# Seven-product couples first, plain couples last, in the down projections of a two-layer encoder kernel

## The chip, the cores and the metric

One core of one Trainium2 chip runs the whole kernel. The metric is the time of one execution on the device, in microseconds (us); lower is better. TensorE (PE in the profile) multiplies matrices and writes to PSUM banks, VectorE (DVE) and ScalarE (ACT) do elementwise work, GpSimd (POOL) a little of it, and SyncE (SP) issues nearly all transfers between memory and the chip's buffers.

## What is computed

A block of 256 tokens by 2048 features goes through two layers. Each is a normalisation, a token mixer (mLSTM in layer 1, HGRN2 in layer 2), a residual addition, then a second normalisation, a gated feed-forward network 5504 wide, and a residual addition. The reference's feed-forward part, which is the part that the change touches:

```
def conv_glu(hn, w_up, conv_w, conv_b, w_down):
    u = hn @ w_up
    a, v = jnp.split(u, 2, axis=-1)
    s = a.shape[1]
    pad = CONV_W // 2
    ap = jnp.pad(a, ((0, 0), (pad, pad), (0, 0)))
    c = conv_b
    for j in range(CONV_W):
        c = c + ap[:, j:j + s] * conv_w[j]
    return (jax.nn.gelu(c, approximate=False) * v) @ w_down
...
        h = h + mix
        h = h + conv_glu(rmsnorm(h, norm_ffn_g[layer]), ffn_w_up[layer], ffn_conv_w[layer],
                         ffn_conv_b[layer], ffn_w_down[layer])
```

All data is float32. The last matrix product, by `w_down` (5504 by 2048), is the down projection.

## The kernel before, in words

**Split weights.** No matrix product is made of plain float32. Every piece of weights (128 partitions by up to 1024 columns) is turned into two: ACT casts it to a high part `wh` (line 147) and DVE subtracts that from the original to give a low part `wl` (line 148). The activations are split the same way (`g` holds a high and a low half). One product of two 128-row blocks is then three matmuls: high by high, high by low, low by high. Lines 357 and 361 are the matmuls of the up projection, line 236 those of the down projection. The weight parts of the down projection live in four buffers of one pool and two of a second (`WB`, `MORE`).

**Stages of a feed-forward network.** The 43 blocks of 128 hidden features are done in two parts, 22 and 21. A part first makes its up blocks (`done_up`, lines 1189 to 1215): after the matmuls of one up block ACT and DVE take its two results out of the `mm` banks into a tile `avc` of 1536 columns, do the convolution and the GELU, and write the split activation `g0`, `g1`, ... (its last step is line 1207). Then comes the down projection of that part as two *pairs*, one after the other; a pair is two chunks of 512 output columns, 1024 in all, and is summed over all of the part's hidden blocks. So there are four places where up blocks end and a first pair begins (two layers by two parts), and at each of them the last `g` tiles are still being made while the pair begins.

**Couples.** A pair goes through its hidden blocks two at a time, in *couples* numbered from 0. A couple is a product of two-by-two blocks: activations A11, A21, A12, A22 (two halves of the tokens, two hidden blocks) by weights B11, B12, B21, B22 (128 by 512 each). A *plain* couple makes all eight products, 24 matmuls, and adds them in four PSUM banks, C11, C12, C21, C22 (`pc` in the profile). A *seven-product* couple makes seven products, 21 matmuls, in Strassen's way: C11, C12 and C21 get one or two products each, and four further banks P1, P6, P7, P5 (`mm` in the profile) one each. It needs sums of token halves (`sx`, made when the second `g` of the couple is done) and combined weights T1, T2, T3, T4. `SEVEN` (line 50) says which couples are seven-product ones; before, couple 0 is plain in every pair, couples 1 and up are seven-product ones, and the last one to three are plain again (in the second part of a network the very last holds a single block). After the last seven-product couple `mid` (line 581) adds the P banks to the residual, by six DVE and two POOL operations; after the pair `done` adds the C banks.

**Where combined weights come from.** For most couples `prepare` (line 613) makes them well ahead, beside the up blocks, and stores them in memory (`tscr`). A pair then loads such a stored couple in three transfers, all issued by SP: 1536 columns of plain weights into a `raw` tile (line 135; 3 buffers), 1536 columns of combined weights into a tile `T` (line 198), and the last 512 into the rest of the `raw` tile (line 199). The couples in `FLY` (one each in three of the four places, none in the last) are combined by four DVE subtractions in place instead (`combine`). The tile `T` has the tag `avc`: it shares three buffers (`TEMP`) with the `avc` tiles of the up blocks. So a `T` transfer waits until the last reader of the tile that used its buffer before is done, be that another `T` (its last reader is the split of its 512-column piece) or an `avc` tile (its last reader is line 1207).

**What sets the order.** The code is written as generators: `split_squares` (line 187) yields the pieces of a pair (cast and split), `squares_by_seven` (line 225) takes them and issues matmuls, a few pieces apart (`LOOK`). A scheduler of the framework then puts the instructions of each engine in an order of its own, by a simulated timeline; few of them are pinned. SP's transfers are issued in the order in which they stand, so one that waits holds up those behind it.

Of the kernel before, what the change touches and what calls it, by code (L numbers as in the profile page):

```python
# [16 lines left out]
T = 256  # L17
# [32 lines left out]
SEVEN = ((1, 2, 3, 4, 5, 6, 7, 8, 9), (1, 2, 3, 4, 5, 6, 7, 8)), ((1, 2, 3, 4, 5, 6, 7, 8, 9), (1, 2, 3, 4, 5, 6, 7))  # L50
# [16 lines left out]
def trunk_kernel(ctx, tc, xT, x_d, fg_d, pp_d, cst_d, w_gate, w_first, w_aq, w_ak, w_av, w_ao, w_aout, w_ao2,  # L67
# [70 lines left out]
    def split_weights(chunks):  # L138

        def parts(r, m, pin=lambda ins: ins, more=None):  # L140
            where, bufs = wpool, WB
            if more is not None:
                turns["w"] += 1
                if turns["w"] % 3 == 0:
                    where, bufs = more, MORE
            wh, wl = (where.tile([P, 1024], F32R, tag=n, bufs=bufs, name=n) for n in ("wh", "wl"))
            pin(act.copy(wh[:, :m], r))  # L147
            pin(dve.tensor_tensor(wl[:, :m], r, wh[:, :m].bitcast(F32), ALU.subtract))  # L148
            return wh, wl
# [33 lines left out]
    def temporary(pool_, name):  # L183
        ff = pool_.name == "ff"
        return pool_.tile([P, 1536], F32, tag="avc" if ff else name, bufs=TEMP if ff else 2, name=name)

    def split_squares(ch, parts):

        units, raws, kept = (ch.nk + 1) // 2, {}, {}
        side.until(lambda: all(ch.waits))  # L190

        def raw(u):
            if u not in raws and u < units:
                n = 1536 if u in ch.stored else min(2048, 1024 * ch.nk - 2048 * u)
                raws[u] = load_raw(ch.src, 2048 * u, 2048 * u + n)
                if u in ch.stored:
                    kept[u] = temporary(ch.pool, "T")
                    nc.sync.dma_start(kept[u], ch.stored[u][:, 0:1536])
                    nc.sync.dma_start(raws[u][:, 1536:2048], ch.stored[u][:, 1536:2048])
            return raws.get(u)  # L200

        def combine(u):
            r, T = raw(u), temporary(ch.pool, "T")
            B11, B22, B21, B12 = (r[:, j * 512:(j + 1) * 512] for j in range(4))
            T2, T3, T4 = (T[:, j * 512:(j + 1) * 512] for j in range(3))
            for x, y, out in ((B12, B22, T3), (B12, B11, B12), (B22, B12, T2), (B21, T2, T4)):
                dve.tensor_tensor(out, x, y, ALU.subtract)
            kept[u] = T

        for u in range(units):  # L210
# [14 lines left out]
    def squares_by_seven(ch, fetch, ready):  # L225
# [19 lines left out]
        def ending(u0):  # L245
            while len(ready) < ch.nk - 2 * u0:
                fetch()
            for t in range(2):
                c, todo, left = (C11, C12, C21, C22)[2 * t:2 * t + 2], [], iter(ready)
                for k in range(2 * u0, ch.nk, 2):  # L250
                    p, x0 = next(left)[:2], half(ch.x(k), t)
                    todo += [(0, x0, block(p, 0))]
                    if k + 1 == ch.nk:
                        todo += [(1, x0, block(p, 1))]
                        break
                    q, x1 = next(left)[:2], half(ch.x(k + 1), t)
                    todo += [(1, x1, block(p, 1)), (0, x1, block(q, 0)), (1, x0, block(q, 1))]
# [16 lines left out]
        for u in range(units):  # L274
# [26 lines left out]
            B11, B22 = block(p[:2], 0), block(p[:2], 1)  # L301
            if u in ch.seven:
                S1, S3, S2, S4 = ch.sums(u)
                products((P1, A11, B11), (C12, S4, B22))
                T2, T3 = piece()
                products((P6, S2, T2), (P7, S3, T3))
                B21, T1 = piece()
                products((C11, A12, B21), (P5, S1, T1))
                T4, _ = piece()
                products((C21, A22, T4))  # L310
                if u == last:
                    ch.mid(psm_)
                    ch.rest = ch.ends
                continue
            B21, B12 = piece()
# [259 lines left out]
    def pair(src, nk, c0, x, sums, norm, seven):  # L575
# [34 lines left out]
        ch.stored, ch.waits, ch.pool, ch.ends, ch.rest = {}, (), None, False, False  # L610
        return ch

    def prepare(tiles, todo, first, period, finished, start, ahead):
# [12 lines left out]
        for i, (_, dst) in enumerate(todo):  # L626
# [3 lines left out]
            B11, B22, B21, B12 = (loaded[i][j // 2][:, j % 2 * 512:(j % 2 + 1) * 512] for j in range(4))  # L630
# [544 lines left out]
    def ffn(layer, norm, nxt):  # L1175
# [40 lines left out]
        for part, (f0, nf) in enumerate(((0, FA), (FA, FB))):  # L1216
# [15 lines left out]
            def two(src, c0, norm, seven, fly, shares, GT=GT, SX=SX, nf=nf):  # L1232
# [8 lines left out]
                assert not left  # L1241
                pairs.append(ch)
# [70 lines left out]
def layout(x, norm_mix_g, norm_ffn_g, mlstm_w_in, mlstm_b_gate, mlstm_head_g, mlstm_w_out, hgrn_w_in, hgrn_lb,  # L1313
# [69 lines left out]
```

## Time and profile before

| what | value |
|---|---|
| timed runs, us | 2366.45, 2367.96, 2375.84; median 2367.96 |
| span of the profiled execution, us | 2364.5; the fastest timed run is 1.95 above it, the median 3.46 |
| PE busy, us (share of the span) | 2354.1 (100%) |
| weight loads on PE | 2016.2 (85%) |
| DVE | 1993.5 (84%) |
| ACT | 1470.0 (62%) |
| POOL | 196.5 (8%) |
| bytes moved | 632.97 MB, mean 268 GB/s |
| granted TensorE clock in the page's slices | 9 tenths or more in all 40 |

The profile is of one execution, and its times are microseconds from the start of its span. It cannot be compared to a tenth with the timed runs, but its own stretches can with one another. In a timeline row stand the start, the busy time, the engine, the line, the operation and the tiles that it writes and reads; a number in square brackets at the end is how long the engine sat idle before it, and what ended that. A matmul of 512 columns is shown some 0.39 us long, but its successor starts about 0.227 us after it, since matmuls overlap; the distance of the starts is what counts. The four places at which a first pair begins are at 634.29 and 975.12 (layer 1), and 1909.32 and 2250.33 (layer 2); they are called L1a, L1b, L2a and L2b here.

### The profile page before, as it was taken

What the parts mean: (1) busy time and instruction counts of PE and PEld (TensorE: products, weight loads), DVE (VectorE), ACT (ScalarE), POOL (GpSimd) and SP (SyncE); (2) the same over time, 40 slices, a digit from 0 to 9 for tenths busy, and PEclk for the clock granted to TensorE, in tenths of its full rate; (3) what the DMA queues carried; (4) which work ended last, traced back from release to release, by engine and by line L of the source; (5) the groups of instructions that cost most, each with busy time, mean ns of one, the idle gap of its engine ahead of it and who ended that gap; (6) DMA issues with size and microseconds to landing.
All of it is one profiled execution on the core that took longest, in us unless ns stands there. A gap on an engine that the chain in (4) does not pass through costs nothing. (4 is left out here: it accounts for less than half of the span.)

```text
span 2364.5 us, 38407 instructions
## 1 busy us (share of the span) xinstructions
PE 2354.1 (100%) x14545; PEld 2016.2 (85%) x14545; DVE 1993.5 (84%) x3087; ACT 1470.0 (62%) x2340; POOL 196.5 (8%) x244
## 2 busy tenths in 40 slices
PE   9999999999999999999999999999999999999998
PEld 8888888888888888888888888888888888888887
DVE  7777687888998898897888888778789889888888
ACT  7655456555665555676777777776555567455565
POOL 0100000000000000000232322220000000000000
PEclk9999999999999999999999999999999999999999
DMA  8776656888888878996556665646788888888896
GB/s 303 239 248 242 213 195 211 295 282 292 313 321 327 306 282 292 330 334 230 208 203 223 212 225 204 214 169 228 270 300 289 289 321 335 295 287 302 309 351 221
DMA packets 122266, 632.97 MB, mean 268 GB/s; under 512 B 13776, under 2 KB 14928, under 8 KB 77664
## 3 DMA queue, kind: packets, MB, share of 16 engines
q1 hardware_dynamic: 120384, 626.51, 75.0%
q0 software_dynamic: 1120, 3.21, 0.8%
q8 instruction: 114, 1.87, 0.3%
q10 hardware_dynamic: 576, 0.79, 0.1%
q14 instruction: 72, 0.59, 0.1%
HBM read 562.24 MB, written 68.22 MB: 267 GB/s over the span
## 5 line engine op out<-in xcount | busy, mean ns | idle before, releaser
L357 PE MATMUL mm<-xt,wh 128*128 128x512 f32 x3776 | 1312.0, 394 | 0.0
L148 DVE TENSOR_TENSOR wl<-raw,wh 128x1024 fp32r<-128x1024 f32 (+1 forms) x844 | 1037.3, 1234 | 222.6 <-ACT wh L147 214.5
L147 ACT CAST wh<-raw 128x1024 fp32r<-128x1024 f32 (+1 forms) x844 | 875.3, 1042 | 513.0 <-PE mm L357 305.8
L361 PE MATMUL mm<-xt,wl 128*128 128x256 f32 x3776 | 1043.5, 278 | 0.0
L357 PEld LDWEIGHTS mm<-xt,wh 128*128 128x128 f32 x3776 | 705.6, 188 | 160.6 <-issue 0.4
L361 PEld LDWEIGHTS mm<-xt,wl 128*128 128x128 f32 x3776 | 709.4, 188 | 4.5
L373 PE MATMUL mm<-wh,xt 128*128 128x512 f32 x1024 | 324.4, 392 | 0.6 <-ACT wh L147 0.5
L236 PE MATMUL pc<-wh,g 128*128 128x512 f32 (+1 forms) x716 | 243.2, 388 | 0.3 <-ACT wh L147 0.2
L373 PEld LDWEIGHTS mm<-wh,xt 128*128 128x128 f32 x1024 | 191.2, 188 | 40.0 <-ACT wh L147 1.1
L632 DVE TENSOR_TENSOR praw<-praw 128x512 f32<-128x512 f32 x252 | 174.1, 691 | 44.7 <-DMA praw<-in_w_d 29.0
L373 PE MATMUL mm<-wl,xt 128*128 128x512 f32 x512 | 199.7, 391 | 0.0
L236 PEld LDWEIGHTS pc<-wh,g 128*128 128x128 f32 x716 | 134.1, 188 | 29.0 <-ACT wh L147 1.5
L236 PE MATMUL mm<-wh,sx 128*128 128x512 f32 x432 | 153.4, 389 | 0.0
L148 DVE TENSOR_TENSOR wl<-T,wh 128x1024 fp32r<-128x1024 f32 (+1 forms) x144 | 135.9, 955 | 13.3 <-ACT wh L147 8.9
L147 ACT CAST wh<-T 128x1024 fp32r<-128x1024 f32 (+1 forms) x144 | 118.6, 835 | 44.7 <-DMA T<-tscr 18.2
L236 PE MATMUL pc<-wl,g 128*128 128x512 f32 (+1 forms) x358 | 138.8, 388 | 0.0
L591 POOL TENSOR_TENSOR hm<-hm,u 128x512 f32<-128x512 f32 x10 | 14.8, 1481 | 1223.8 <-DVE u L590 1223.8
L373 PEld LDWEIGHTS mm<-wl,xt 128*128 128x128 f32 x512 | 96.2, 188 | 18.6
L1071 DVE TENSOR_TENSOR QK<-QK,G 128x256 f32<-128x256 f32 x224 | 104.6, 515 | 6.2 <-ACT kq L1050 5.9
L1195 ACT COPY avc<-mm 128x256 f32<-128x256 f32 x172 | 64.0, 372 | 63.9 <-PE mm L361 63.6
L1050 ACT COPY kq<-QK 128x512 f32<-128x512 f32 x112 | 74.5, 669 | 37.3 <-DVE QK L1071 29.5
L236 PEld LDWEIGHTS mm<-wh,sx 128*128 128x128 f32 x432 | 81.0, 188 | 16.9 <-ACT wh L147 0.2
(246 smaller groups left out, 2263.1 us busy)
## 6 DMA issues: line engine op xcount, KB each, us to landing
raw<-in_w_up SPq DMA_DIRECT2D x172, 1024.0 KB, 6.1
tscr<-praw SPq DMA_DIRECT2D x126, 512.0 KB, 6.7
praw<-in_w_d SPq DMA_DIRECT2D x120, 512.0 KB, 6.8
raw<-in_w_bq SPq DMA_DIRECT2D x48, 1024.0 KB, 5.0
T<-tscr SPq DMA_DIRECT2D x63, 768.0 KB, 7.6
raw<-in_w_d SPq DMA_DIRECT2D x60, 768.0 KB, 6.0
raw<-in_w_ao SPq DMA_DIRECT2D x24, 1024.0 KB, 4.8
raw<-in_w_d SPq DMA_DIRECT2D x24, 1024.0 KB, 7.7
```

The lines of the kernel that those rows point to most:

```text
L147: pin(act.copy(wh[:, :m], r))
L148: pin(dve.tensor_tensor(wl[:, :m], r, wh[:, :m].bitcast(F32), ALU.subtract))
L236: pin(pe.matmul(ps, a, b, start=bank not in begun, stop=stop and i == 2))
L357: hold(pe.matmul(ps[f], wh[:, c:c + P], x, start=k + kk == 0, stop=False))
L361: hold(pe.matmul(ps[f][:, 0:T], wl[:, c:c + P], x[:, 0:T], start=False, stop=k + kk == ch.nk - 1))
L373: pe.matmul(ps[t], x[:, a + t * P:a + (t + 1) * P], w[:, c], start=st and i == 0, stop=sp and i == 2)
L591: pool.tensor_tensor(part(1, 0), part(1, 0), u, ALU.add)
L632: dve.tensor_tensor(out, x, y, ALU.subtract)
L1050: act.copy(m, blocks(QK, h))
L1071: dve.tensor_tensor(two[:, j], two[:, j], by[:, j], ALU.mult)
L1195: act.copy(z, p[:, T:2 * T])
```

## The change

It does four things at once; the number of couples of each kind stays what it was, and each engine has as many instructions as before.

1. `SEVEN` names couples 0 to 8, 0 to 7, 0 to 8 and 0 to 6 in place of 1 to 9, 1 to 8, 1 to 9 and 1 to 7: a pair begins with seven-product couples and ends with plain ones.
2. The four weight blocks of a couple are stored in the order B12, B11, B22, B21 (before: B11, B22, B21, B12), and so the pieces of a seven-product couple come in another order. The first piece is now (B21, T4), for the products into C11 and C21 (`outer`); then (B11, B22) for C12 and P1, then (T2, T3) for P6 and P7, then T1 alone for P5. The first piece lies wholly in the `raw` tile, of which the last 512 columns are now loaded ahead of the tile `T`.
3. In the second pair of each place (`c0` not zero) the first couple has `lead`: it does P1, P6, P7 and P5 first, then C12, and `outer` last. So this pair begins in the `mm` banks and not in the `pc` banks that the first pair's `done` has still to read.
4. The ending of the last pair goes through its two blocks in another order.

The diff, cut to its core:

```
-SEVEN = ((1, 2, 3, 4, 5, 6, 7, 8, 9), (1, 2, 3, 4, 5, 6, 7, 8)), ((1, 2, 3, 4, 5, 6, 7, 8, 9), (1, 2, 3, 4, 5, 6, 7))
+SEVEN = (tuple(range(9)), tuple(range(8))), (tuple(range(9)), tuple(range(7)))
...
         def raw(u):
             if u not in raws and u < units:
-                n = 1536 if u in ch.stored else min(2048, 1024 * ch.nk - 2048 * u)
-                raws[u] = load_raw(ch.src, 2048 * u, 2048 * u + n)
+                o = 2048 * u + 512 * (u in ch.stored)
+                raws[u] = load_raw(ch.src, o, min(2048 * (u + 1), 1024 * ch.nk))
                 if u in ch.stored:
                     kept[u] = temporary(ch.pool, "T")
+                    nc.sync.dma_start(raws[u][:, 1536:2048], ch.stored[u][:, 1536:2048])
                     nc.sync.dma_start(kept[u], ch.stored[u][:, 0:1536])
-                    nc.sync.dma_start(raws[u][:, 1536:2048], ch.stored[u][:, 1536:2048])
             return raws.get(u)
...
         for u in range(units):
-            r = raw(u)
-            yield *parts(r[:, 0:1024], 1024, more=ch.pool), 1
-            if u + 1 in ch.seven and u + 1 not in ch.stored:
-                combine(u + 1)
+            r, todo = raw(u), []
             if u in ch.seven:
-                yield *parts(kept[u][:, 0:1024], 1024, more=ch.pool), 1
-            if 2 * u + 1 < ch.nk:
-                yield *parts(r[:, 1024:2048], 1024, more=ch.pool), 1
-            if u in ch.seven:
-                yield *parts(kept[u][:, 1024:1536], 512, more=ch.pool), 1
+                T = kept[u]
+                todo = [(r[:, 1024:2048], 1024), (r[:, 0:1024], 1024)] if u in ch.stored else \
+                    [(outer(r), 1024), (r[:, 512:1536], 1024)]
+                todo += [(T[:, 512:1536], 1024), (T[:, 0:512], 512)]
+                if u in ch.lead:
+                    todo.append(todo.pop(0))
+            else:
+                todo = [(r[:, o:o + 1024], 1024) for o in (0, 1024)[:1 + (2 * u + 1 < ch.nk)]]
+            for i, (w, m) in enumerate(todo):
+                yield *parts(w, m, more=ch.pool), 1
+                if i == 0 and u + 1 in ch.seven and u + 1 not in ch.stored:
+                    combine(u + 1)
...
             if u in ch.seven:
                 S1, S3, S2, S4 = ch.sums(u)
-                products((P1, A11, B11), (C12, S4, B22))
-                T2, T3 = piece()
-                products((P6, S2, T2), (P7, S3, T3))
-                B21, T1 = piece()
-                products((C11, A12, B21), (P5, S1, T1))
-                T4, _ = piece()
-                products((C21, A22, T4))
+                lead = u in ch.lead
+
+                def outer(a, b):
+                    T4, B21 = (b, a) if u in ch.stored else (a, b)
+                    products((C11, A12, B21), (C21, A22, T4))
+                if not lead:
+                    outer(a, b)
+                    a, b = piece()
+                    products((C12, S4, b))
+                products((P1, A11, a))
+                products(*zip((P6, P7), (S2, S3), piece()))
+                products((P5, S1, piece()[0]))
                 if u == last:
                     ch.mid(psm_)
                     ch.rest = ch.ends
+                if lead:
+                    products((C12, S4, b))
+                    outer(*piece())
                 continue
...
-        ch.stored, ch.waits, ch.pool, ch.ends, ch.rest = {}, (), None, False, False
+        ch.stored, ch.waits, ch.pool, ch.ends, ch.rest, ch.lead = {}, (), None, False, False, ()
...
+                ch.lead = (0,) if c0 else ()
                 pairs.append(ch)
...
-        w = np.stack([w[:, 0, :, 0], w[:, 1, :, 1], w[:, 1, :, 0], w[:, 0, :, 1]], axis=2)
+        w = np.stack([w[:, 0, :, 1], w[:, 0, :, 0], w[:, 1, :, 1], w[:, 1, :, 0]], axis=2)
```

How the instructions stand is shown at three places. The first is SP at the beginning of the down projection at L2b. `in_w_d0` are the plain weights of the first pair, `raw_22968` is the raw tile of couple 0, and the `L635` rows (after: `L653`) are stores of combined weights for the second pair. Before, `T_23012` belongs to couple 1 and `T_23109` to couple 2:

```order
L135 DMA raw_22968<-in_w_d0 128x2048
L635 DMA tscr<-praw_22863 128x1024
L135 DMA raw_23010<-in_w_d0 128x1536
L199 DMA raw_23010<-tscr 128x512
L635 DMA tscr<-praw_22864 128x1024
L198 DMA T_23012<-tscr 128x1536
L135 DMA raw_23107<-in_w_d0 128x1536
L199 DMA raw_23107<-tscr 128x512
L135 DMA raw_23149<-in_w_d0 128x1536
L199 DMA raw_23149<-tscr 128x512
L135 DMA raw_23191<-in_w_d0 128x1536
L198 DMA T_23109<-tscr 128x1536
```

After, `T_22970` belongs to couple 0 and `T_23075` to couple 1:

```order
L135 DMA raw_22968<-in_w_d0 128x1536
L201 DMA raw_22968<-tscr 128x512
L653 DMA tscr<-praw_22863 128x1024
L653 DMA tscr<-praw_22864 128x1024
L135 DMA raw_23073<-in_w_d0 128x1536
L201 DMA raw_23073<-tscr 128x512
L202 DMA T_22970<-tscr 128x1536
L135 DMA raw_23115<-in_w_d0 128x1536
L201 DMA raw_23115<-tscr 128x512
L135 DMA raw_23157<-in_w_d0 128x1536
L201 DMA raw_23157<-tscr 128x512
L202 DMA T_23075<-tscr 128x1536
```

In each the first `T` goes at about the same place, and the second five or six transfers later; what has moved is which couples they belong to, 1 and 2 before, 0 and 1 after.

The second place is DVE at the same point of the program. Before, the rows from the split of the first piece of couple 1's `T` on; `g19` and `g20` are the last two activations, `avc_23035` is the tile of the last up block, and the rows with `raw_23107` are the split of couple 2's first piece:

```order
L148 TENSOR_TENSOR wl_23066<-T_23012,wh_23065 128x1024
L148 TENSOR_TENSOR wl_23070<-raw_23010,wh_23069 128x1024
L1207 TENSOR_TENSOR g19_22927<-avc_22916,g19_22927 128x256
L1196 TENSOR_TENSOR avc_23035<-mm_22930,avc_23035 128x256
L148 TENSOR_TENSOR wl_23098<-T_23012,wh_23097 128x512
...
L148 TENSOR_TENSOR wl_23113<-raw_23107,wh_23112 128x1024
L1207 TENSOR_TENSOR g20_23046<-avc_23035,g20_23046 128x256
L148 TENSOR_TENSOR wl_23123<-T_23109,wh_23122 128x1024
```

After, from the split of the first piece of couple 0's `T` on:

```order
L151 TENSOR_TENSOR wl_23014<-T_22970,wh_23013 128x1024
L151 TENSOR_TENSOR wl_23064<-T_22970,wh_23063 128x512
L151 TENSOR_TENSOR wl_23079<-raw_23073,wh_23078 128x1024
L1225 TENSOR_TENSOR g19_22927<-avc_22916,g19_22927 128x256
...
L1225 TENSOR_TENSOR g20_23044<-avc_23033,g20_23044 128x256
L151 TENSOR_TENSOR wl_23099<-T_23075,wh_23098 128x1024
L151 TENSOR_TENSOR wl_23106<-T_23075,wh_23105 128x512
L151 TENSOR_TENSOR wl_23121<-raw_23115,wh_23120 128x1024
```

Here couple 0's `T` is split in two rows with nothing between, and then no `T` is split until the last activation `g20` is done; in the program as built the transfer of `T_23075` (couple 1) waits for the row that writes `wl_23064`, the last reader of `T_22970`, whose buffer it takes, and in L1a, L1b and L2a the couple 1 transfer waits likewise for the 512-column split of couple 0's `T`.

The third place is PE where the second pair follows the first at L1a. Before, the last three rows of the first pair and the first of the second:

```order
L236 MATMUL pc_6320<-wh_6703,g21_6310 128x512
L236 MATMUL pc_6320<-wl_6704,g21_6310 128x512
L236 MATMUL pc_6320<-wh_6703,g21_6310 128x512
L236 MATMUL pc_6787<-wh_6725,g0_4006 128x512
L236 MATMUL pc_6787<-wl_6726,g0_4006 128x512
```

After, the same place:

```order
L246 MATMUL pc_6318<-wl_6709,g21_6308 128x512
L246 MATMUL pc_6318<-wh_6708,g21_6308 128x512
L246 MATMUL mm_6781<-wh_6717,g0_4006 128x512
L246 MATMUL mm_6782<-wh_6745,sx_4113 128x512
L246 MATMUL mm_6782<-wl_6746,sx_4113 128x512
```

The second pair now writes to an `mm` bank first and needs token sums (`sx_4113`) and a piece of a `T` from its second matmul on, where before it wrote to a `pc` bank and needed only plain weights.

More of the change, by code (lines that the diff above doesn't have):

```diff
@@ L146, in parts @@
             wh, wl = (where.tile([P, 1024], F32R, tag=n, bufs=bufs, name=n) for n in ("wh", "wl"))
-            pin(act.copy(wh[:, :m], r))
-            pin(dve.tensor_tensor(wl[:, :m], r, wh[:, :m].bitcast(F32), ALU.subtract))
+            h, l = wh[:, :m], wl[:, :m]
+            if len(r.shape) == 3:
+                h, l = (z.rearrange("p (b c) -> p b c", b=2) for z in (h, l))
+            pin(act.copy(h, r))
+            pin(dve.tensor_tensor(l, r, h.bitcast(F32), ALU.subtract))
             return wh, wl
@@ L203, in combine, with outer @@
             r, T = raw(u), temporary(ch.pool, "T")
[L204 to L206 removed]
+            B12, B11, B22, B21 = (r[:, j * 512:(j + 1) * 512] for j in range(4))
+            T1, T2, T3 = (T[:, j * 512:(j + 1) * 512] for j in range(3))
+            for x, y, out in ((B12, B22, T3), (B12, B11, T1), (B22, T1, T2), (B21, T2, B12)):
                 dve.tensor_tensor(out, x, y, ALU.subtract)
             kept[u] = T
+        def outer(r):
+            return r.rearrange("p (b c) -> p b c", b=4)[:, 0:4:3]
         for u in range(units):
[L211 to L214 removed]
+            r, todo = raw(u), []
             if u in ch.seven:
[L216 to L220 removed]
+                T = kept[u]
[10 more added lines that the diff above has]
+                    combine(u + 1)
     def banks():
@@ L313, in squares_by_seven @@
                     ch.rest = ch.ends
+                if lead:
+                    products((C12, S4, b))
+                    outer(*piece())
                 continue
-            B21, B12 = piece()
+            B12, B11 = a, b
+            B22, B21 = piece()
             for ps, (x, w), (y, v) in ((C11, (A11, B11), (A12, B21)), (C12, (A11, B12), (A12, B22)),
@@ L629, in prepare @@
                 load(i + 1)
-            B11, B22, B21, B12 = (loaded[i][j // 2][:, j % 2 * 512:(j % 2 + 1) * 512] for j in range(4))
+            B12, B11, B22, B21 = (loaded[i][j // 2][:, j % 2 * 512:(j % 2 + 1) * 512] for j in range(4))
             for x, y, out in ((B12, B22, B22), (B12, B11, B12), (B11, B22, B11), (B21, B11, B21)):
```

7 lines of the change are left out of this document (3 added, 4 removed).

## The prediction

> **What bounds the kernel now.** I read the page's busy times first, then the waits of PE, then the four stretches in which down projections run, then PE's timeline at the places where it lost time, and last the transfers of the tiles `T`. From the page:
>
> ```profile
> PE 2354.1 (100%) x14545; PEld 2016.2 (85%) x14545; DVE 1993.5 (84%) x3087; ACT 1470.0 (62%) x2340; POOL 196.5 (8%) x244
> ```
>
> PE is busy for 2354.1 of 2364.5 us, so nothing can become much faster except by taking matmuls away, and this change takes none away. The waits of PE name the two that a down projection has (line, releaser, total, times, longest):
>
> ```profile
> PE mm L236 <- DVE wl L148: 0.5, 1, 0.5
> ...
> PE pc L236 <- ACT wh L147: 0.2, 1, 0.2
> ```
>
> The table by stage has one row for each place (start and end, length, then PE, weight loads, DVE, ACT and POOL, the granted clock, the DMA share and GB/s):
>
> ```profile
> 634.30:742.20 107.90, 107.83 (x477) 88.91 (x476) 99.29 (x112) 73.08 (x86) 3.54 (x2) 1.00 0.86 321
> 975.10:1080.30 105.20, 105.20 (x474) 87.14 (x472) 98.33 (x111) 74.92 (x96) 7.01 (x4) 1.00 0.82 298
> 1909.30:2017.40 108.10, 107.88 (x477) 88.86 (x476) 102.59 (x117) 73.03 (x87) 3.60 (x3) 1.00 0.88 325
> 2250.30:2356.60 106.30, 105.76 (x479) 87.24 (x477) 92.94 (x111) 69.84 (x89) 7.58 (x5) 1.00 0.78 291
> ```
>
> PE has no gaps worth naming there, at full clock; DVE has only 3 to 13 us of room in a stretch, and the DMA engines are 0.78 to 0.88 busy. The down projections are bound by PE, with DVE and the transfers close behind. Where PE lost anything, its timeline shows it. First L2b, then L2a, L1a and L1b, each with the row in which the first pair starts:
>
> ```profile
> 2250.33 0.40 PE L236 MATMUL pc<-wh,g 128*128 128x512 f32 x1
> ...
> 2260.54 0.49 PE L236 MATMUL mm<-wh,g 128*128 128x512 f32 x1
> 2260.86 0.40 PE L236 MATMUL pc<-wh,g 128*128 128x512 f32 x1
> 2261.79 0.50 PE L236 MATMUL mm<-wl,g 128*128 128x512 f32 x1 [0.53 <-DVE wl L148]
> 2262.13 0.40 PE L236 MATMUL mm<-wh,g 128*128 128x512 f32 x1
> ```
>
> ```profile
> 1909.32 0.39 PE L236 MATMUL pc<-wh,g 128*128 128x512 f32 x1
> ...
> 1930.43 0.69 PE L236 MATMUL mm<-wh,sx 128*128 128x512 f32 x2
> 1931.33 0.50 PE L236 MATMUL pc<-wh,g 128*128 128x512 f32 x1 [0.22 <-ACT wh L147]
> ```
>
> ```profile
> 634.29 0.39 PE L236 MATMUL pc<-wh,g 128*128 128x512 f32 x1
> ...
> 699.59 0.61 PE L236 MATMUL mm<-wh,sx 128*128 128x512 f32 x2
> 700.28 0.50 PE L236 MATMUL pc<-wh,g 128*128 128x512 f32 x1
> ```
>
> ```profile
> 975.12 0.40 PE L236 MATMUL pc<-wh,g 128*128 128x512 f32 x1
> ```
>
> A matmul start follows the one before by 0.227 us where nothing is waited for (687.58 to 687.81 and twice on to 688.26, further below). From 2260.54 to 2262.13 there are three steps, 0.68 at that pace, and 1.59 were taken: 0.9 lost. From 1930.43 to 1931.33 two steps took 0.90, not 0.45: 0.45 lost. From 699.59 to 700.28 two steps took 0.69: 0.24 lost. That is 1.6 us in all, and it is the most that a better order can win back in these stretches.
>
> **The change part by part.**
>
> *Work.* Every engine has as many instructions after as before and the couples of each kind are as many, so matmuls, casts and splits cost nothing more or less. Nine subtractions of on-the-fly couples write another tile of the same size: 0.
>
> *The second pair begins in the product banks.* It saves a wait only if the second pair waits now for the banks that `done` still reads. PE at the switch at L1a (the second pair's first matmul is the second of the x2):
>
> ```profile
> 687.58 0.39 PE L236 MATMUL pc<-wl,g 128*128 128x512 f32 x1
> 687.81 0.62 PE L236 MATMUL pc<-wh,g 128*128 128x512 f32 x2
> 688.26 0.39 PE L236 MATMUL pc<-wl,g 128*128 128x512 f32 x1
> ```
>
> The pace is unbroken, so there is nothing to save: 0. The 0.24 lost at 700, where the second pair's first stored couple begins, can go with the new order, and nothing that I found takes its place, as the second pair's first `T` now has the plain end of the first pair to arrive in: -0.24. Bounds 0 and -0.24 there.
>
> *Seven-product couples first.* This is the part with a price, at the start of the first pair. Before, the 24 matmuls of plain couple 0 need no `T`: 24 x 0.227 = 5.4 us in which the first `T` (couple 1) has time to land and to be split, and the second `T` (couple 2) is needed only another couple later. Now couple 0 needs a `T` after 12 matmuls, and couple 1's after 21 + 12 = 33: 7.48 us after the start. As the program is built, the scheduler puts 2 more ahead at L1b and 6 more at L2a (7.94 and 8.85 us). So couple 1's `T`, cast, is due at 634.29 + 7.48 = 641.77, 975.12 + 7.94 = 983.06, 1909.32 + 8.85 = 1918.17 and 2250.33 + 7.48 = 2257.81.
>
> When can it be there? Its transfer waits for the buffer of the first `T`, that is for the split of that tile's 512 columns. The first `T` itself cannot be loaded sooner than now, because its buffer comes from an `avc` tile of the same up blocks. At L2b it was issued and used so:
>
> ```profile
> 2239.59 0.42 SPq L198 DMA_DIRECT2D T<-tscr  x1
> ```
>
> ```profile
> 2251.58 1.05 ACT L147 CAST wh<-T 128x1024 fp32r<-128x1024 f32 x1 [3.04 <-DMA T<-tscr]
> ```
>
> ```profile
> 2255.61 0.68 DVE L148 TENSOR_TENSOR wl<-T,wh 128x512 fp32r<-128x512 f32 x1
> ```
>
> It landed at 2251.5, 11.9 after its issue (the longest of the landing times below). Cast until 2252.63 that is 0.4 before couple 0's need at 2250.33 + 12 x 0.227 = 2253.05, so couple 0 hardly waits. Its 512 columns were split by 2256.29; now that split stands right behind the one of the 1024, so it can end at about 2251.58 + 1.05 + 1.3 + 0.68 = 2254.6. Couple 1's transfer is issued between 2254.6 and 2256.3. The other places have these rows, in each the split or the transfer that frees a `T` buffer first, and the `g` row (L1207) that frees the next buffer:
>
> ```profile
> 1909.92 0.69 DVE L148 TENSOR_TENSOR wl<-T,wh 128x512 fp32r<-128x512 f32 x1
> ...
> 1915.38 0.42 DVE L1207 TENSOR_TENSOR g<-avc,g 128x256 fp32r<-128x256 f32 x1
> ```
>
> ```profile
> 977.22 0.32 SPq L198 DMA_DIRECT2D T<-tscr  x1
> ```
>
> ```profile
> 979.24 0.42 DVE L1207 TENSOR_TENSOR g<-avc,g 128x256 fp32r<-128x256 f32 x1
> ```
>
> ```profile
> 635.14 0.68 DVE L148 TENSOR_TENSOR wl<-T,wh 128x512 fp32r<-128x512 f32 x1
> 636.08 0.41 DVE L1207 TENSOR_TENSOR g<-avc,g 128x256 fp32r<-128x256 f32 x1
> ```
>
> Issue is thus at 1910.6 to 1915.8 (L2a), 977.2 to 979.7 (L1b) and 635.2 to 636.5 (L1a, the split at most 0.6 sooner). The time from issue to landing of the `T` transfers around each start (minimum, median, maximum of three), L1a, L1b, L2a, L2b:
>
> ```profile
> DMA to landing us min/median/max: 5.2/6.4/7.5
> ```
>
> ```profile
> DMA to landing us min/median/max: 4.3/7.6/9.2
> ```
>
> ```profile
> DMA to landing us min/median/max: 6.1/6.4/6.8
> ```
>
> ```profile
> DMA to landing us min/median/max: 5.9/7.8/11.9
> ```
>
> Issue, plus the smallest time of landing for the early end and the median for the late end (the largest, 6.8, at L2a), plus the cast of 1.05, less the due time:
>
> - L2b: 2261.55 to 2265.15, late by 3.7 to 7.3; middle 5.5. The 0.9 lost at 2260.5 is replaced by this: +4.6.
> - L2a: 1917.75 to 1923.65, late by 0 to 5.5 (0.4 early at best); middle of -0.4 and 5.5: 2.5. The 0.45 is replaced: +2.1.
> - L1b: 982.55 to 988.35, late by 0 to 5.3; middle 2.4.
> - L1a: 641.45 to 643.95, late by 0 to 2.2; middle 0.9.
>
> I take middles, since no row shows whether the scheduler's place for the split or the load on the queues wins. What is queued behind the waiting `T` transfer on SP is couple 2's `T` and later raw tiles; couple 2's is due 21 matmuls (4.8 us) after couple 1's, so it does not add. On DVE the two splits of that `T` hold up the split of couple 2's first piece, which costs nothing while PE itself stands.
>
> A row about transfers and a rule: the `T` transfers of 768 KB took 5.9 us and more at L2b. The Trainium skill, "DMA: Bandwidth & Descriptors", section Bandwidth, gives 6.15 us measured for 1 MB by itself; scaled to 768 KB that is an estimate of 4.6 us. By that page the four would be late by 3.3, 0.7, 1.0 and 0 from the middle of the issue times, and the sum would be +3.4, not +9.8. Here the queues are 0.78 to 0.88 busy and the trace's times stand.
>
> Sum: 4.6 + 2.1 + 2.4 + 0.9 - 0.24 = +9.8 us on the profiled execution, 2364.5 to 2374.3. The median of the runs is 3.46 above that span, and the same is taken for after: 2367.96 + 9.8 = 2377.8. Bounds: all early, 3.7 - 0.9 - 0.45 - 0.24 = +2.1; all late, 7.3 + 5.5 + 5.3 + 2.2 - 1.6 = +18.7.
>
> **The rivals.** A run of this kernel can tell some 0.5% from no change, 11.8 us: under 2356.1 is faster, over 2379.8 slower.
>
> *R1, slower: the clock drops in the long stalls.* All prices above are at full clock. The end of the trace shows what standing still does (the last matmul, and two stretches of 1 us after it):
>
> ```profile
> 2356.30 0.28 PE L236 MATMUL rest<-wh,g 128*128 128x256 f32 x1
> ```
>
> ```profile
> 2360.00:2361.00 1.00, 0.00 (x0) 0.00 (x0) 0.00 (x0) 0.00 (x0) 0.00 (x0) 1.00 0.81 267
> 2361.00:2362.00 1.00, 0.00 (x0) 0.00 (x0) 0.00 (x0) 0.00 (x0) 0.00 (x0) 0.50 1.03 368
> ```
>
> PE stood from 2356.58, and 4.4 us later the granted clock was 0.50. L2b's stall of 5.5 is over that, and L2a's upper half too. No row shows how long the clock stays low once work is back; if as long as it took to fall, 4.4 us at half speed lose 2.2. With both: 9.8 + 2 x 2.2 = +14.2, 2382.2. It decides from an unbroken stall of about 4.4 us. Against it: the stall may come in two pieces, couple 0's `T` having its low part late by half a microsecond first.
>
> The Trainium skill, "TensorE: Matmul & The Clock Gate", Part 1, has a rule that speaks against this change: an idle window of about 3.4 us halves the clock, and some 3.4 us of work are needed to get it back. The trace's 4.4 us agree as far as 1 us stretches can show. By that page one such stall costs 1.7 us of lost work, and the sum would be +11.5 with L2b's alone.
>
> *R2, slower: all four transfers at the late ends.* +18.7, 2386.7. For it: the first `T` at L2b took 11.9. Against it: four independent places.
>
> *R3, no change with a small gain: the loads are in time.* If the new order lets the first `T` be issued and split earlier, no stall arises and the 1.6 us are won: 2366.4. For it: at three places the early end is on time. Against it: L2b is late by 3.7 at best.
>
> *That the change does not do what it says:* starting in the product banks frees no wait, as the switch showed; that is in the sum already.
>
> **How the numbers follow.** The forecast (stalls of +2 to +11.8) gets 0.56; R3 0.14; R1 0.18; R2 0.10; a gain over 0.5% by something unseen 0.02, as PE has 2354.1 us of matmuls either way. Hence faster 0.02, same 0.56 + 0.14 = 0.70, slower 0.28. The range reaches from just under R3 (2366.0) past R1 to 2383.5; it leaves out R2, the unseen gain and the upper tail of R1, somewhat under 0.2.
>
> **What would show it right or wrong.** In the profile after: at each first pair's start, about 33 to 39 matmuls in, PE should wait for a `wh` or `wl` made from `T`, longest at L2b (near 5.5 us) and least at L1a; the wait of ACT for the `T` transfer should stand right beside it; the switch between the pairs should run at 0.227 us as before; the granted clock in the microseconds behind L2b's stall tells R1 from the forecast. The forecast is wrong if PE waits under 2 us in all at the four starts (R3), if couple 1's `T` is issued well before couple 0's is split, or if time appears where up blocks, mixers or second pairs run.

## The result, and the profile after

The changed kernel takes 2385.57 us (median of 6 runs, 2381.53 to 2388.96), the kernel before 2367.64 in the runs beside it; the ratio is 1.0072, 95% interval 1.0058 to 1.0085. That is 17.9 us slower, past the 11.8 us that were called a clear difference, and above the predicted range (2366.0 to 2383.5). The profiled execution has a span of 2384.0 us, 19.5 more than before. Its page, the busy times:

```profile
PE 2363.5 (99%) x14545; PEld 2018.2 (85%) x14545; DVE 1995.7 (84%) x3087; ACT 1469.2 (62%) x2340; POOL 196.1 (8%) x244
```

The work is the same; PE is shown 9 us busier because matmuls at half clock, and those around a wait, are shown longer. What PE waited for (line, releaser, total, times, longest):

```profile
PE mm L246 <- ACT wh L150: 5.1, 5, 3.0
PE pc L246 <- ACT wh L150: 3.6, 4, 1.7
PE mm L246 <- DVE wl L151: 1.7, 4, 0.7
...
PE pc L246 <- DVE wl L151: 0.8, 2, 0.5
```

That is 11.2 us in place of 0.7, all of it for weight parts of the down projection. The table by stage, each row from the first matmul of a place to its last:

```profile
634.30:746.90 112.60, 110.44 (x478) 89.93 (x477) 103.63 (x115) 73.73 (x86) 7.71 (x4) 0.98 0.85 317
979.60:1088.10 108.50, 107.22 (x474) 86.20 (x473) 102.13 (x116) 76.20 (x101) 7.97 (x4) 1.00 0.79 285
1917.10:2033.60 116.50, 111.70 (x477) 89.65 (x476) 103.93 (x116) 73.52 (x89) 6.90 (x4) 0.99 0.83 309
2266.30:2376.10 109.80, 106.78 (x479) 88.27 (x477) 94.58 (x113) 69.89 (x90) 7.54 (x5) 0.98 0.76 278
```

Beside the 107.90, 105.20, 108.10 and 106.30 of before these are 4.7, 3.3, 8.4 and 3.5 us longer, 19.9 in all, which is the whole loss; and the clock is no longer 1.00 in three of them. L2b's worst place, in PE's timeline:

```profile
2273.60 0.39 PE L246 MATMUL mm<-wh,sx 128*128 128x512 f32 x1
2276.95 1.22 PE L246 MATMUL mm<-wh,sx 128*128 128x512 f32 x2 [2.96 <-ACT wh L150]
2277.55 1.05 PE L246 MATMUL mm<-wh,sx 128*128 128x512 f32 x2
2278.40 0.63 PE L246 MATMUL mm<-wl,sx 128*128 128x512 f32 x1
2278.82 0.63 PE L246 MATMUL mm<-wh,sx 128*128 128x512 f32 x1
```

PE stands for 2.96 us, 7.3 us after the pair's start (2266.33), just where couple 1's `T` is due; then the steps are 0.42 and not 0.227. The same microseconds in a table of stretches, with the granted clock as the third number from the right:

```profile
2275.00:2276.00 1.00, 0.00 (x0) 0.00 (x0) 0.44 (x2) 0.51 (x3) 0.00 (x0) 1.00 0.83 332
2276.00:2277.00 1.00, 0.05 (x1) 0.05 (x1) 0.48 (x2) 1.00 (x2) 0.00 (x0) 0.75 0.98 410
2277.00:2278.00 1.00, 1.00 (x3) 0.78 (x3) 1.00 (x1) 1.00 (x2) 0.00 (x0) 0.50 1.03 373
...
2280.00:2281.00 1.00, 1.00 (x6) 0.81 (x5) 1.00 (x2) 1.00 (x3) 0.00 (x0) 1.00 1.03 236
```

The clock halved while PE still stood, at 2276.50, and stayed so until 2279.91, for 3.4 us. The next table adds up, place by place, by how much the matmul starts stood further apart than 0.227 us (steps more than 0.06 over; clusters under 0.4 left out):

| where, us after the first pair's start | lost, us | of it half-speed steps x 0.2 |
|---|---|---|
| L1a, +7.5 | 0.7 | 0 |
| L1a, second pair, +65 | 4.1 | 7 |
| L1b, +7.3 | 1.3 | 0 |
| L1b, +26.5 | 1.3 | 0 |
| L2a, +7.3 | 4.1 | 7 |
| L2a, +25.7 | 1.7 | 0 |
| L2a, second pair, +68 | 2.8 | 0 |
| L2b, +7.3 | 4.6 | 5 |

In all 20.6; before, the same count gives 1.7. With the clusters under 0.4 it is 21.3 and 2.2.

### The profile page after: what moved, and what is told of

It reads as the page before. It is cut to its first block, busy times and chain, and to the rows that moved or that the text cites. A ratio compares the mean times of both kernels' runs of the same rounds, so it can differ in the third digit from the quotient of the medians.

```text
span 2384.0 us, 38375 instructions
## 1 busy us (share of the span) xinstructions
PE 2363.5 (99%) x14545; PEld 2018.2 (85%) x14545; DVE 1995.7 (84%) x3087; ACT 1469.2 (62%) x2340; POOL 196.1 (8%) x244
## 4 chain that ended last, share of the span: by engine, by line
PE 91%; DMA 4%; DVE 3%; issue 1%; ACT 1%; SPq 0%; DVEq 0%; POOLq 0%; POOL 0%; ACTq 0%
PE mm L375 34%; PE mm L391 18%; PE mm L379 17%; PE pc L246 11%; PE mm L246 7%; DMA T<-tscr 3%; DVE wl L151 2%; PE pn L867 1%; ACT wh L150 1%; DMA praw<-in_w_d 1%; PE py L1126 1%; PE pd L1076 0%; PE pz L452 0%; PE pa L1076 0%; DMA raw<-in_w_first 0%
## 5 line engine op out<-in xcount | busy, mean ns | idle before, releaser
L151 DVE TENSOR_TENSOR wl<-T,wh 128x512 fp32r<-128x512 f32 (+1 forms) x144 | 137.5, 982 | 23.1 <-ACT wh L150 22.8
L150 ACT CAST wh<-T 128x512 fp32r<-128x512 f32 (+1 forms) x144 | 116.8, 833 | 61.5 <-DMA T<-tscr 28.4
L246 PEld LDWEIGHTS mm<-wh,sx 128*128 128x128 f32 x432 | 81.9, 191 | 25.7 <-ACT wh L150 9.2
```

Source lines behind the costliest of these rows:

```text
L150: pin(act.copy(h, r))
L151: pin(dve.tensor_tensor(l, r, h.bitcast(F32), ALU.subtract))
L246: pin(pe.matmul(ps, a, b, start=bank not in begun, stop=stop and i == 2))
```

## The experiments

Each kernel was timed in three rounds; the ratio is to the kernel before in the same rounds (2367.1 to 2367.6). "Lost" is always counted as in the table above, from one profiled execution of each kernel; where one number is given for a whole place, the clusters under 0.4 are in it. Theory A is the prediction's: couple 1's `T` lands late, because its buffer is that of couple 0's `T`. Theory B came from the profile after: the first piece of an on-the-fly couple is now (B21,T4), and T4 is the last of four subtractions.

**e1: the old list of couples.**

```
-SEVEN = (tuple(range(9)), tuple(range(8))), (tuple(range(9)), tuple(range(7)))
+SEVEN = ((1, 2, 3, 4, 5, 6, 7, 8, 9), (1, 2, 3, 4, 5, 6, 7, 8)), ((1, 2, 3, 4, 5, 6, 7, 8, 9), (1, 2, 3, 4, 5, 6, 7))
```

> The changed kernel with the old list of seven-product couples (1 to 9 and so on, so couple 0 is plain and `lead` never applies); the new block and piece order stays. Theory A (the T of couple 1 is late at the start of first pairs, because it takes the buffer of couple 0's T): those stalls go, time within 3 us of before, 2367 to 2371. Theory B (the first piece of an on-the-fly couple is now (B21,T4), so its cast needs the whole chain of four subtractions, which DVE finishes too late): the on-the-fly couples still stall, 3 to 8 us over before, 2371 to 2376. If both hold, near 2371 to 2374. A third theory, that the new piece order is harmful everywhere, gives over 2378.

Measured: 2369.85 us, ratio 1.0011 (1.0001 to 1.0021). The stalls at the starts and at the on-the-fly couples are gone, but for 0.4 at L2b, +13.4, and 0.5 where L1a's second pair begins; a new 2.2 is lost at L2b's end, in two waits for low parts, and its cause is open. So the new blocks and pieces cost some 2.5 us by themselves; all the rest comes with the seven-product couples standing first, through whichever theory: behind a plain couple 0 the on-the-fly couples no longer stall either.

**e2: the new list alone.** The same line, changed in the kernel before.

> The kernel before with nothing but the new list of couples (0 to 8 and so on); old block order, old pieces, no lead. Theory A: the late T of couple 1 remains, and it is due 6 matmuls (1.4 us) sooner, as the piece (T2,T3) comes second: 11 to 17 us over before, 2379 to 2385. Theory B: the stalls at on-the-fly couples are gone, since their first piece is plain; alone it would give 2368 to 2371.

Measured: 2381.70 us, ratio 1.0061 (1.0046 to 1.0076): 14.3 us over before, so most of the loss needs neither new pieces nor `lead`. It loses 5.0, 2.7, 2.7 and 7.2 us at the four places. 4.2 of L2b's 7.2 and 2.2 of L1a's 5.0 stand at couple 1's `T`, as theory A has it; another 2.9 at L2b stand around couple 0's, which landed 1.1 us after the pair's start. At L1b and L2a nothing over 0.4 is lost in the first 15 us. Theory B's expectation was not wholly met: with the plain piece first, 0.8 and 1.6 are still lost at the on-the-fly couples of the second pairs at L1a (+69) and L2a (+66), where ACT waits 3.68 and 4.17 us for a subtraction.

**e3: on-the-fly couples with the plain piece first.**

```
-                ch.lead = (0,) if c0 else ()
+                ch.lead = ((0,) if c0 else ()) + fly
```

> The changed kernel with the on-the-fly couples done in the order of `lead` too: plain piece (B11,B22) first, (B21,T4) last. Theory B: the stalls at couple 2 of the second pair at L1a (4.1 us with the slow clock), at couple 5 at L1b (1.2) and at couple 2 of the second pair at L2a (2.8) go, 6 to 8 us less than the changed kernel, 2377 to 2380; at L2a's first pair the stall at 1924 stays, since couple 1's T is late there as well. Theory A alone: no change, 2384 to 2387.

Measured: 2378.58 us, ratio 1.0049 (1.0034 to 1.0064), 7.0 us less than the changed kernel. Theory B holds for that much. The 4.1 at L1a's second pair became 1.3, L1b's 1.3 became 0.7 and L2a's 2.8 went; a new 0.9 came at L1a, +78, behind a transfer. One expectation was wrong: the 4.1 at L2a's start, which was put down to couple 1's `T`, fell to 0.4; that was an on-the-fly couple too, couple 2, whose cast the scheduler had put ahead. At L1a's second pair the wait that was 1.70 us long in the changed kernel is 0.54 in e3:

```profile
702.56 0.73 PE L246 MATMUL pc<-wh,g 128*128 128x512 f32 x2 [0.54 <-ACT wh L150]
```

What B is, the changed kernel shows at L1a's second pair, on PE, then DVE (L210 are the subtractions), then ACT:

```profile
699.49 0.39 PE L246 MATMUL mm<-wh,g 128*128 128x512 f32 x1
701.57 0.73 PE L246 MATMUL pc<-wh,g 128*128 128x512 f32 x2 [1.70 <-ACT wh L150]
```

```profile
694.73 1.28 DVE L210 TENSOR_TENSOR T<-raw 128x512 f32<-128x512 f32 x2
...
698.20 0.68 DVE L210 TENSOR_TENSOR T<-raw,T 128x512 f32<-128x512 f32 x1
698.92 0.69 DVE L210 TENSOR_TENSOR raw<-raw,T 128x512 f32<-128x512 f32 x1
```

```profile
700.48 1.04 ACT L150 CAST wh<-raw 128x1024 fp32r<-128x1024 f32 x1
```

The four subtractions run from 694.73 to 699.61, with splits between; the cast of the piece with T4 can only then begin, ends at 701.52, and PE goes on at 701.57.

**e5: no `lead`.**

```
-                ch.lead = (0,) if c0 else ()
+                ch.lead = ()
```

> The changed kernel without `lead`: the second pair begins with (B21,T4) into the C banks like the first. The prediction's step (beginning in the product banks saves no wait): within 1 us of the changed kernel, 2384.5 to 2386.5. Rival (with seven-product couples first, the second pair would wait for the C banks that `done` still reads, 4 additions of 0.6 us): 2 to 4 us slower at each of four places at most, 2388 to 2398.

Measured: 2386.51 us, ratio 1.0080 (1.0065 to 1.0095), the same as the changed kernel within the interval. Beginning the second pair in the product banks saves nothing that can be measured.

**e6: couple 1 plain in place of couple 0** (on e3).

```
-SEVEN = (tuple(range(9)), tuple(range(8))), (tuple(range(9)), tuple(range(7)))
+SEVEN = ((0, *range(2, 10)), (0, *range(2, 9))), ((0, *range(2, 10)), (0, *range(2, 8)))
```

> The kernel of e3 (on-the-fly couples in the order of `lead`) with couple 1 plain in place of couple 0: seven-product couples 0, 2 to 9 and so on, as many as before. The second stored T is now due 5.4 us later. Theory A (couple 1's T comes late, because of the buffer that it takes): the stalls 7 to 12 us after the start of first pairs go (1.1, 0.6, 0.4 and 5.2 in e3), some 6 us less than e3's 2378.6: 2371 to 2374. Rival (the first pair begins too full for DVE and the transfers, whichever T comes): the stalls only move on to the next couples, 2376 to 2379.

Measured: 2372.60 us, ratio 1.0022 (1.0012 to 1.0032), 6.0 less than e3. The stalls 7 to 12 us after the starts are gone, L2b loses 1.7 in place of 5.9. So it is couple 1's `T` that is late at the starts, but not yet why. L2a now loses 4.5 at +24, with seven half-speed steps.

**e7 and e8: three and four buffers** (on e3, with seven seven-product couples in each pair, which makes 30 more matmuls in all; the last two lines are e8's alone).

```
-SEVEN = (tuple(range(9)), tuple(range(8))), (tuple(range(9)), tuple(range(7)))
+SEVEN = (tuple(range(7)),) * 2, (tuple(range(7)),) * 2
-TEMP = 3
+TEMP = 4
```

> The kernel of e3 with seven-product couples 0 to 6 in all four places (five couples fewer, so 10 x 3 matmuls of 0.227 us more: +6.8 us of work), which makes room for another T buffer in the next kernel. It is the reference for that one: e3's 2378.6 + 6.8 = 2385, less what a shorter run of seven-product couples saves in stalls further on, 2381 to 2386.

> The kernel of e7 with four buffers for T and avc tiles in place of three, so that couple 1's T waits for no split of couple 0's T. Theory A: couple 1's T lands in time, the stalls 7 to 12 us after the start of first pairs go, 5 to 8 us less than e7, nearly all of it at L2b and L1a. Rival (the transfer rate sets when that T lands, whatever the buffer): within 2 us of e7, with PE still waiting at the same places.

Measured: e7 2376.44 us (ratio 1.0036, 1.0024 to 1.0048), e8 2376.96 us (1.0038, 1.0023 to 1.0053). e7 came out lower than expected: with the shorter lists nothing is lost at L1a and L1b, even with three buffers. At L2b's start e7 loses 2.2, and e8 4.3: theory A, as it stood, has fallen. e8's rows at L2b show two reasons. SP issued couple 1's `T` early, but it took 10.1 us to land, and ACT cast it late:

```profile
2254.12 0.43 SPq L202 DMA_DIRECT2D T<-tscr  x1
```

```profile
DMA to landing us min/median/max: 10.1/10.1/10.1
```

```profile
2264.32 0.60 ACT L1218 ACTIVATE avc<-avc,pp 128x256 f32<-128x256 f32 x1 [2.63 <-DVE avc L1216]
...
2266.05 0.42 ACT L1221 ACTIVATE avc<-avc 128x256 f32<-128x256 f32 x1 [0.20 <-DVE avc L1220]
2267.48 0.41 ACT L1224 CAST g<-avc 128x256 fp32r<-128x256 f32 x1 [1.01 <-DVE avc L1222]
2267.79 1.56 ACT L150 CAST wh<-T 128x1024 fp32r<-128x1024 f32 x2
```

The `T` was there at 2264.2, and its cast began at 2267.79. On ACT it stands behind the last up block's convolution, GELU and split, three instructions that themselves wait for DVE; ACT is idle for 2.63 + 0.20 + 1.01 = 3.8 us in them. This is theory C. The landing itself came no sooner than in e7: 7.9 us after the pair's start (2256.34), in e7 7.5, where the `T` was issued some 5 us later against the start and took 4.6. So the rival named ahead of e8, that the rate of the transfers sets the landing, is not excluded. And only 1.4 of e8's 4.3 stand at this cast; 1.8 stand just before, where a cast of plain weights (2264.83) is held by the same chain, and the rest earlier. In the changed kernel ACT's queue is the same:

```profile
2268.90 1.79 SPq L202 DMA_DIRECT2D T<-tscr  x2
```

```profile
DMA to landing us min/median/max: 4.6/4.6/4.6
```

```profile
2274.64 0.42 ACT L1221 ACTIVATE avc<-avc 128x256 f32<-128x256 f32 x1 [1.13 <-DVE avc L1220]
2275.55 0.40 ACT L1224 CAST g<-avc 128x256 fp32r<-128x256 f32 x1 [0.49 <-DVE avc L1222]
2275.86 1.56 ACT L150 CAST wh<-T 128x1024 fp32r<-128x1024 f32 x2
```

It landed at 2273.5 and was cast from 2275.86.

**e9: that chain behind the cast** (on e3). The convolution of a part's last up block, and what follows it, is emitted some couples later, and `ins`, the convolution, is ordered behind `mark[0]`, the cast of couple 1's `T`.

```
+                    if f in (FA - 1, FA + FB - 1):
+                        tc.add_manual_dep(ins.ins, mark[0],
+                                          mybir.DependencyInfo(mybir.DependencyClass.NoSync, mybir.DependencyReason.DATA),
+                                          reason="order")
```

> The kernel of e3 with one order changed: the convolution, GELU and split of the last up block of each part stand on ACT behind the cast of couple 1's T, where they stood ahead of it (nothing left out). Theory C (at L2b couple 1's T has landed and its cast waits in ACT's queue behind that chain, which itself waits for DVE): L2b's stall of 5.2 us with its slow spell shrinks to the 0.7 or so that the landing leaves, 3 to 5 us less than e3's 2378.6, 2373.5 to 2376; the small stalls at L1a and L1b, whose casts start right when T lands, stay. Theory A (the landing of that T): no change, 2377 to 2380. A third: the avc buffer that is held longer delays the T tiles after it, and the stall only moves some couples on, 2377 to 2381.

Measured: 2377.97 us, ratio 1.0049 (1.0032 to 1.0066), as e3. L2b's loss falls from 5.9 to 4.0 and its half-speed steps go, but now ACT waits for the transfer there:

```profile
2268.14 1.56 ACT L151 CAST wh<-T 128x1024 fp32r<-128x1024 f32 x2 [5.01 <-DMA T<-tscr]
```

And what L2b gains is lost again at L1b and L2a (3.7 and 3.5 in place of 2.1 and 2.2); the `avc` buffer that is held longer, as the third theory said, may be the reason. The edit moves the chain's instructions on DVE behind as well, so it does not tell ACT's queue from DVE's. Neither A nor C alone is enough: theory D says both.

**e10 and e11: e7 and e8 with e9's order.** The two edits above together.

> The kernel of e7 (seven-product couples 0 to 6, three buffers) with the last up block's convolution, GELU and split put behind the cast of couple 1's T on ACT, as in e9. Theory D (at L2b two things are late about together, the landing of couple 1's T, because of the buffer, and its cast, because of the chain in ACT's queue, so that taking one away leaves the other): the stall at L2b, 2.2 us in e7, stays within 1 us of that. Theory C alone: it goes. In time: within 2 us of e7's 2376.4 by either, so the profile decides.

> The kernel of e8 (seven-product couples 0 to 6, four buffers) with the same order on ACT: both causes are taken away. Theory D: PE no longer waits for a cast of couple 1's T at L2b, the 4.3 us that e8 lost there falls under 1.5, 2372.5 to 2375. Rival (the first pair at L2b begins too full for DVE and the transfers, whatever stands ahead in a queue): 3 us or more stay, in other waits, 2376 to 2378.

Measured: e10 2375.93 us (ratio 1.0037, 1.0024 to 1.0050), e11 2373.77 us (1.0025, 1.0015 to 1.0036). Lost at L2b:

| | three buffers | four buffers |
|---|---|---|
| chain ahead of the cast | 2.2 (e7) | 5.3 (e8) |
| cast ahead of the chain | 3.5 (e10) | 0.0 (e11) |

Only with both changed does the stall go. e10's 3.5 is 1.3 more than e7's 2.2, where at most 1 was expected.

The table holds more than theory D, though. In e8 and e10 couple 0's `T` landed 0.9 and 1.3 us after the pair's start, in e7 and e11 1.2 and 1.1 before it, and a part of 5.3 and 3.5 is lost by that, before couple 1 is reached. At couple 1's `T` alone the loss is 1.4 (e7), 1.4 (e8), 1.2 (e10) and 0.0 (e11). How much of e10's 1.2 the buffer causes and how much that late landing, through the split that frees the buffer, is not told apart.

The profile of e11 is its fastest run (2372.16), so the stall may not be wholly gone in the others; but the medians agree that either edit alone changes nothing clear of noise and both together some 2.7 us (e7 to e11, with intervals that overlap). ACT in e10, then in e11:

```profile
2266.84 1.57 ACT L151 CAST wh<-T 128x1024 fp32r<-128x1024 f32 x2 [2.81 <-DMA T<-tscr]
```

```profile
2263.89 1.57 ACT L151 CAST wh<-T 128x1024 fp32r<-128x1024 f32 x2 [1.00 <-DMA T<-tscr]
2265.37 0.60 ACT L1228 ACTIVATE avc<-avc,pp 128x256 f32<-128x256 f32 x1
```

And e11's stretch of L2b:

```profile
2256.80:2362.00 105.20, 105.17 (x479) 87.47 (x477) 93.95 (x112) 69.47 (x90) 7.55 (x5) 1.00 0.78 291
```

PE is busy for 105.17 of 105.20 us at full clock. e11 is 6.2 us over before in the same rounds and has 10 x 3 x 0.227 = 6.8 us more matmuls: with these orders and buffers, and seven of them to a pair, seven-product couples first cost nothing and win nothing that could be measured. No version that was run beats the kernel before; there is no room for four buffers beside the full lists, so that version was not tried.

## Why the prediction was wrong

- *PE bounds the kernel, and 1.6 us at most can be won:* right. Every loss is a place where PE stands or runs at half clock, and e11 ends about where the count of matmuls says (6.2 over before, 6.8 counted).
- *The product banks save no wait:* right (e5). At the switch at L1a the rows after are as even as those before:

```profile
688.38 0.39 PE L246 MATMUL pc<-wl,g 128*128 128x512 f32 x1
688.61 0.39 PE L246 MATMUL pc<-wh,g 128*128 128x512 f32 x1
688.83 0.39 PE L246 MATMUL mm<-wh,g 128*128 128x512 f32 x1
689.06 0.39 PE L246 MATMUL mm<-wh,sx 128*128 128x512 f32 x1
```

- *"Nine subtractions of on-the-fly couples write another tile of the same size: 0", and at the second pair "nothing that I found takes its place":* this is the step that failed, and the sign that the prediction named, time in the second pairs, came with it. The subtractions cost the same (two in each of nine couples write another tile), but the fourth now makes half of the couple's first piece, where before the first piece was plain and the chain had the whole of it as cover. I counted instructions and did not ask which product needs the last of them. It cost 4.1 us at L1a's second pair, where -0.24 had been forecast, 2.8 at L2a's second and 1.3 at L1b, and most of L2a's 4.1 at the start. e3 wins back 7.0 us by that order alone, and its 2378.58 lies inside the range. Where a plain couple 0 stands first (e1) the same order of pieces shows no such stall, and with the old order behind a seven-product couple 0 (e2) 2.4 us are lost at these couples, so it is the two changes together that cost so much.
- *Couple 1's `T` late at four starts, +0.9, +2.4, +2.5, +5.5:* the places were right, and 0.7, 1.3, 4.1 and 4.6 were lost, but only at L1a, and for some 0.8 of L1b's 1.3, for the reason given. There the cast begins as the `T` lands (at L1b the transfer issued at 983.05 took 4.6 and the cast began at 987.65). L2a's was the on-the-fly couple; at L2b the buffer is one of two causes that run side by side, and the other, the chain in ACT's queue, was visible in the order of the instructions, where no `T` is split until `g20` is done. I read the row for DVE and did not price the wait on ACT. From these rows, as an estimate: `T` landed at 2273.55, so its cast could have ended at 2274.60, 0.8 after PE was ready for it (2273.83); the queue made it 2276.91, 2.3 more. That 4.6 was forecast and 4.6 lost at L2b is luck, and so is the sum of the four starts (10.0 forecast, 10.7 less the 1.7 of before measured).
- *Landing times of 5.9 to 7.8 at L2b:* too long for the start; couple 1's `T` took 4.6 there, and 5.6, 4.6 and 6.5 at L1a, L1b and L2a. The 4.6 that was estimated for a transfer by itself was met at two places.
- *R1, the clock:* it did fall, at three places, for 19 half-speed steps of 0.2 us, 3.8 us in all. The price of one spell (2.2 forecast, 1.0 to 1.4 measured) was near; its threshold, an unbroken 4.4 us, was wrong (see the last section).
- *R2:* its size was met by luck (+18.7, measured +17.9), not its cause. The range ended below the result because on-the-fly couples had no term in it.

Left open: the 1.7 at L2a, +25.7. The `T` there was issued at 1932.40 and took 10.4 us to land (PE waited 0.84 us for its cast), with the DMA engines at 1.02 and 424 GB/s in the microsecond in which PE stood. That the transfer rate is the limit there was argued and not tried.

## What to carry to other kernels

When an order is turned round, ask of each piece not what it costs but which step of its making comes last, and whether the piece that used to be the cover still stands ahead of it. A step that waits in an in-order queue can be held by what stands ahead of it there as well as by its own data; if taking away one cause changes nothing, take away both before calling the theory false. Stalls in a kernel that is bound by PE cost more than they last, as the clock may drop in them.

## What the runs showed of the hardware

The clock fell after much shorter waits than the 4.4 us at the end of the trace, and not by length alone. At L1a PE waited 1.70 us, then in smaller pieces, and ran at half clock from about 703:

```profile
700.00:701.00 1.00, 0.00 (x0) 0.00 (x0) 0.91 (x1) 1.00 (x3) 0.00 (x0) 1.00 0.80 307
701.00:702.00 1.00, 0.43 (x2) 0.30 (x2) 1.00 (x3) 1.00 (x2) 0.00 (x0) 1.00 0.56 233
702.00:703.00 1.00, 0.79 (x4) 0.30 (x2) 1.00 (x2) 1.00 (x3) 0.00 (x0) 0.98 0.11 43
703.00:704.00 1.00, 1.00 (x4) 0.83 (x3) 1.00 (x2) 0.94 (x1) 0.00 (x0) 0.50 0.00 0
```

Here it fell only when PE was at work again; at L2b it fell while PE still stood. In e5 a step of the same 1.86 us beyond pace at the same place brought no half-speed step, and in e9 L2b lost 3.2 us in one cluster without any.

The traces show what decides. In the changed kernel the three spells begin at 702.95, 1928.34 and 2276.50, and the granted clock is halved for 3.41 to 3.42 us in each. The distances between their beginnings, 1225.39 and 348.16, are 359 and 102 times 3.413: the clock changes only at the ends of equal stretches of 3.41 us that run on through the whole execution. Take 0.227 us of work for each matmul of 512 columns. The stretches that end at these three falls held 0.95, 1.19 and 0.74 us of work. Of all stretches at full clock between 20 and 2350 us in the twelve profiles, those with at most 1.38 us of work (eight, in five profiles) all ended in a fall, and none with 1.52 or more did, so the limit, as an estimate from these counts, lies at some 40 to 45% of a stretch. e5's stall lay across two stretches, with 1.90 us of work in the first, and so did e9's, with 1.75 and 1.82. The Trainium skill, "TensorE: Matmul & The Clock Gate", Part 1, says that a window of some 3.4 us that does not start with the kernel's own work decides; that the same stall costs a spell in one run and none in another agrees with it, and so do spells of 3.4 us. The table of that part speaks of an idle window; here a stretch with up to 1.38 us of work was enough, and the measurement decides.
